# The S5 stretch of a hybrid diffusion layer, issued to TensorE in a written order

## The chip, the cores and the metric

The kernel runs on one core of a Trainium2 chip. Times are device microseconds of one execution. The kernel before took 1824.79 us, the median of 3 runs (1820.09 to 1827.46). A core has TensorE (PE, matrix products), VectorE (DVE), ScalarE (ACT), GpSimd (POOL) and SyncE (SP, which issues the transfers); each engine executes its own queue in order, and they wait for each other by semaphores.

## The reference, cut to what matters

One layer of a diffusion backbone over 256 context tokens and 512 latent tokens, width 1024, all in float32. One projection feeds three mixers:

```
hc, h = norm(context), norm(latent)             # (256, 1024), (512, 1024)
proj  = h @ w_in        # u (S5) | q,k,v | beta, decay | z | conv value, conv gate | gates
u     : s5_scans(u)     # 64 groups x 64 complex states, both directions, context then latent
        y = Re(C h) + d*u ; gelu(y) * sigmoid(gelu(y) @ w_glu)
q,k,v : silu(conv of 3 taps); q,k divided by their norm; gated delta rule, chunks of 64, both directions
conv  : value*sigmoid(gate); conv of 31 taps; layernorm; silu
merged = sum of three sigmoid gates * (branch @ w_br) ; x + g1 * (merged @ w_out)
then a ConvGLU feed-forward and a last norm
```

The context rows need only the states of S5 and the delta rule, so of u, q, k, v there are 768 columns (512 + 256), of conv 512.

## The kernel before, in words

Matrices are kept transposed: 128 channels on the partitions, tokens along the row. `proj` (L406) makes 128 channels: it loads 8 weight tiles, splits them into a high and a low part (`split`, high on ACT L181, low on DVE or POOL L185), and `mm3` runs 24 matmuls (L206 to L208) into one PSUM bank; with the context another 24 of 256 columns follow.

S5 is handled in 8 blocks of 8 groups. For a block:

- `s5_u` projects u (on PE) and sends it to DRAM; `s5_in` reads it back as `s5U`.
- `s5_in` makes input weights on DVE (`cmul`, L170 to L175, each 128x1024), transposes them on PE (L600, copied by ACT L602), multiplies them with `s5U` (L610) and has ACT copy the result to `s5VH` (L612 to L614); K matmuls (L628) and two transposes (L634) make the local kernel, which goes to DRAM.
- `s5_phase` and `s5_scan` run on GpSimd: the phase table (`s5ph`, powers by doubling), six products over 128x768 (L648, `s5G`), 16 scans on DVE (L658), six products over 128x512 (`s5H`). The tables `s5ph`, `s5G`, `s5H`, `s5pt` have one buffer each, so the loop of the blocks is closed on GpSimd.
- `s5_y` makes output weights on DVE (L686 to L691), copies H (ACT L694, L695) and runs 8 x (1 matmul of L699, 2 of L702); the page counts each of the 24 as two records.

Behind the stretch of S5 the program has `dn_gates` (the decay gates, a long chain of small DVE operations between its transposes, L1068, and its sums, L1109), `conv_in` (for each of 8 channel tiles two projections and `conv_taps`: 32 matmuls, 64 records, L939, with four loads of `cv_y` and a weight tile that GpSimd makes) and `dn_pre` (for each of 8 heads: K, Q, V by `proj`, `dn_silu` on DVE and ACT, transposes L1165, L1176, L1193, norms). Then the delta rule begins (`dn_head`, first matmul L1240); it is filled up with `jobs` (L738 to L743), projections that are cut in single matmuls.

The order on each engine is not the order of the code: a scheduler places every instruction by priority (code order) and readiness. Projections of later blocks and of `dn_pre` so come between the S5 steps wherever the scheduler found room. Buffers come from pools: `dn_th` (two buffers) holds silu's temporaries, and the conv input `cv_t` too, whose edges GpSimd clears (L888, L889).

Of the kernel before, what the change touches and what calls it, by code (L numbers as in the profile page):

```python
# [16 lines left out]
P = 128  # L17
# [62 lines left out]
class Kern:  # L80
# [337 lines left out]
    def s5_u(self, m, pool):  # L418
# [6 lines left out]
        nc.sync.dma_start(self.u_d[m], st.rearrange("p j n -> p (j n)"))  # L425

# [143 lines left out]
    def s5_in(self, blk, NG=8):  # L570
# [5 lines left out]
        U = bp.tile([P, NG, 96], F32, name="s5U")  # L576
        ud = self.u_d[blk]
        for j in range(8):
            nc.sync.dma_start(
                U[16 * j:16 * j + 16],  # L580
                bass.AP(tensor=ud.tensor, offset=ud.offset + j * 96, ap=[[768, 16], [16 * 768, NG], [1, 96]]))
# [11 lines left out]
        self.cmul(w[0], w[1], bv[0], bv[1], av[0], av[1], t)  # L593
        WT = []
# [9 lines left out]
        VH = bp.tile([P, 2, NG, 96], F32, name="s5VH", tag="s5VH", bufs=2)  # L604
# [11 lines left out]
        zd = self.dp.tile([240, 16 * NG], F32, name=f"z_d{blk}")  # L616
# [14 lines left out]
        nc.scalar.activation(kt.rearrange("p h f -> p (h f)"), ps[:, :2 * P], AF.Copy)  # L631
        ps = self.psum(tag="s5")
# [8 lines left out]
        return U, VH, zd  # L641

    def s5_scan(self, blk, st, T, NG=8):
# [3 lines left out]
        VH = st[1]  # L647
# [12 lines left out]
        H = self.s5b.tile([P, 2, NG, 64], F32, name="s5H", bufs=1)  # L660
# [7 lines left out]
        return H  # L668

    def s5_y(self, blk, st, H, NG=8):  # L670

        nc, V = self.nc, self.nc.vector
        U, _, z = st
# [17 lines left out]
        V.tensor_tensor(w[1], w[1], t, op=OP.subtract)  # L691

# [181 lines left out]
    def conv_in(self, pool, cvp):  # L874

# [6 lines left out]
        self.conv_weights(cvp)  # L882
        for m in range(KT):
            yield
# [5 lines left out]
            nc.scalar.activation(mid, pg, AF.Tanh, scale=0.5)  # L890
            pa = self.proj(COL_CV + m * P)
# [4 lines left out]
        yield  # L896
        self.conv_taps(KT - 1, cvp)
        nc.sync.dma_start(self.sm_d, self.cv_sm)
# [150 lines left out]
    def dn_gates(self, pool):  # L1049
# [4 lines left out]
        self.rq = cp.tile([P, HEADS, NX], F32, name="rq")  # L1054
        self.rqx = cp.tile([P, HEADS, NX], F32, name="rqx")
# [60 lines left out]
    def dn_silu(self, part, h, pool, c0, out=None):  # L1116
# [17 lines left out]
        V.tensor_scalar(a, raw[:, a0:W], w(0), None, op0=OP.mult)  # L1134
# [14 lines left out]
    def dn_pre(self, h, pool):  # L1149
# [5 lines left out]
        cols = lambda n: self.psum(tag="aux")[:, :n * P].rearrange("p (c f) -> p c f", f=P)  # L1155
        kqt = pool.tile([P, 2 * NX, P], F32, name="dn_Hw", tag="dn_Hw", bufs=2)
        kq = kqt.rearrange("p (c a) f -> p c a f", a=2)
        t, th = self.dn_silu(1, h, pool, COL_K)
# [3 lines left out]
        for c0, c1 in halves:  # L1162
            pt = cols(c1 - c0)
            for c in range(c0, c1):
                nc.tensor.transpose(pt[:, c - c0], t[:, self.tok(c)], self.ident)  # L1165
                nc.scalar.activation(th[:, self.tok(c)], pt[:, c - c0], AF.Square, accum_out=x[:, c:c + 1])
            pts.append(pt)
        V.tensor_scalar(x, x, 4.0 * EPS, None, op0=OP.add)
        self.rsqrt(r, x, pool, NCH, h == HEADS - 1)
        kt = pool.tile([P, NCH + NCT, P], F32, name="dn_Hw", tag="dn_Hw", bufs=2)  # L1170
# [9 lines left out]
        t, th = self.dn_silu(0, h, pool, COL_Q, out=kq[:, :, 1])  # L1180
        sq = th[:, NCTX + 1:]
        nc.scalar.activation(sq.rearrange("p (c f) -> p c f", f=P), kq[:, :, 1], AF.Square)
        ps = self.psum(tag="aux")
        for c in range(NX):
            nc.tensor.matmul(ps[:, c:c + 1], sq[:, c * P:(c + 1) * P], self.ones[:, :1], start=True, stop=True)
# [619 lines left out]
```

## Time and profile before

| | |
|---|---|
| median of 3 runs | 1824.79 us (1820.09 to 1827.46) |
| profiled execution | 1821.67 us, span of its instructions 1819.9 us |
| mean granted TensorE clock | 0.939 |
| PE busy | 1650.5 us, 91% of the span |
| DVE, POOL, ACT busy | 1159.9, 819.0, 691.1 us |
| first projection / last matmul of S5 / first matmul of the delta rule | 50 / 570 / 724 us |

Busy time on PE holds matmuls at the lower clock as well, and matmuls overlap: the time that one takes in a stream is the distance of starts, not its duration. A release `<-ACT x` names what ended the idle time ahead of a row.

### The profile page before, as it was taken

What the parts mean: (1) busy time and instruction counts of PE and PEld (TensorE: products, weight loads), DVE (VectorE), ACT (ScalarE), POOL (GpSimd) and SP (SyncE); (2) the same over time, 40 slices, a digit from 0 to 9 for tenths busy, and PEclk for the clock granted to TensorE, in tenths of its full rate; (3) what the DMA queues carried; (4) which work ended last, traced back from release to release, by engine and by line L of the source; (5) the groups of instructions that cost most, each with busy time, mean ns of one, the idle gap of its engine ahead of it and who ended that gap; (6) DMA issues with size and microseconds to landing.
All of it is one profiled execution on the core that took longest, in us unless ns stands there. A gap on an engine that the chain in (4) does not pass through costs nothing.

```text
span 1819.9 us, 25815 instructions
## 1 busy us (share of the span) xinstructions
PE 1650.5 (91%) x9435; PEld 1339.1 (74%) x9435; DVE 1159.9 (64%) x1982; ACT 691.1 (38%) x1398; POOL 819.0 (45%) x978
## 2 busy tenths in 40 slices
PE   7899878898989999988979989999699799999997
PEld 2687767787878366766768878888567688888886
DVE  6746897678886064366776466544245699999424
ACT  4444433543443144333334455444213243334222
POOL 0548886788782323876455445433142111111020
PEclk9899988988899999998988999999889899999999
DMA  8342332333236668777776455656784233333232
GB/s 297 97 108 77 76 100 83 85 98 94 74 104 164 175 180 286 219 221 218 239 240 164 133 177 158 173 178 190 240 287 150 70 105 93 93 99 99 94 97 76
DMA packets 328689, 268.71 MB, mean 148 GB/s; under 512 B 63333, under 2 KB 264818, under 8 KB 328562
## 3 DMA queue, kind: packets, MB, share of 16 engines
q1 hardware_dynamic: 328130, 266.52, 49.4%
q8 instruction: 74, 1.21, 0.3%
q10 hardware_dynamic: 432, 0.54, 0.1%
q14 instruction: 53, 0.43, 0.1%
HBM read 208.62 MB, written 58.39 MB: 147 GB/s over the span
## 4 chain that ended last, share of the span: by engine, by line
PE 39%; DMA 6%; DVE 4%; POOL 2%; ACT 2%; issue 2%; SPq 0%; DVEq 0%; ACTq 0%; POOLq 0%
PE ps_mm L206 5%; PE ps_mm L207 5%; PE ps_mm L208 5%; PE ps_pr L1240 3%; PE ps_acc L1522 3%; PE ps_mm L738 3%; PE ps_mm L743 3%; PE ps_mm L742 3%; PE ps_acc L1523 3%; PE ps_acc L1521 3%; PE ps_inv L1240 2%; DMA adw<-in_ada_w_dram 1%; DVE kkc L1284 1%; POOL dn_tmp L1303 1%; POOL dn_dd L1305 1%
## 5 line engine op out<-in xcount | busy, mean ns | idle before, releaser
L181 ACT ACTIVATE whi<-wraw 128x1024 fp32r<-128x1024 f32 x187 | 196.8, 1055 | 362.0 <-PE ps_mm L207 167.3
L185 DVE TENSOR_TENSOR wlo<-wraw,whi 128x1024 fp32r<-128x1024 f32 x131 | 177.1, 1354 | 184.5 <-ACT whi L181 184.1
L185 POOL TENSOR_TENSOR wlo<-wraw,whi 128x1024 fp32r<-128x1024 f32 x56 | 135.0, 2412 | 160.3 <-ACT whi L181 152.4
L206 PE MATMUL ps_mm<-hxh,whi 128*128 128x512 f32 (+1 forms) x392 | 160.9, 411 | 11.3 <-ACT dn_raw L1126 8.7
L208 PE MATMUL ps_mm<-hxh,wlo 128*128 128x512 f32 (+1 forms) x392 | 158.5, 404 | 3.1 <-DVE wlo L185 3.1
L207 PE MATMUL ps_mm<-hxl,whi 128*128 128x512 f32 (+1 forms) x392 | 159.2, 406 | 0.7 <-POOL hxl L404 0.7
L1620 DVE SCALAR_TENSOR_TENSOR f_acc<-fpad,vec,f_acc 128x512 f32<-128x512 f32 x176 | 152.5, 866 | 3.2
L185 POOL TENSOR_TENSOR hidl<-f_acc,hidh 128x512 fp32r<-128x512 f32 x22 | 36.8, 1672 | 240.8 <-ACT hidh L181 240.8
L206 PE MATMUL ps_mm<-h2h,whi 128*128 128x512 f32 x352 | 137.7, 392 | 0.7 <-ACT h2h L1585 0.7
L207 PE MATMUL ps_mm<-h2l,whi 128*128 128x512 f32 x352 | 137.5, 391 | 0.0
L208 PE MATMUL ps_mm<-h2h,wlo 128*128 128x512 f32 x352 | 137.3, 390 | 0.0
L743 PE MATMUL ps_mm<-hxh,wlo 128*128 128x512 f32 x256 | 104.7, 409 | 3.5 <-POOL wlo L185 3.4
L738 PE MATMUL ps_mm<-hxh,whi 128*128 128x512 f32 x256 | 106.8, 418 | 0.0
L742 PE MATMUL ps_mm<-hxl,whi 128*128 128x512 f32 x256 | 103.2, 403 | 0.0
L206 PEld LDWEIGHTS ps_mm<-hxh,whi 128*128 128x128 f32 (+1 forms) x392 | 76.0, 194 | 27.3 <-ACT dn_raw L1126 9.2
L208 PEld LDWEIGHTS ps_mm<-hxh,wlo 128*128 128x128 f32 (+1 forms) x392 | 75.4, 192 | 21.2 <-DVE wlo L185 3.7
L207 PEld LDWEIGHTS ps_mm<-hxl,whi 128*128 128x128 f32 (+1 forms) x392 | 75.9, 194 | 15.5 <-POOL hxl L404 1.2
L702 PE MATMUL ps_s<-s5HB,s5w 128*128 128x64 f32 x256 | 57.2, 360 | 28.5 <-DVE s5w L691 20.0
L742 PE MATMUL ps_mm<-xl,whi 128*128 128x512 f32 x192 | 77.8, 405 | 0.8 <-DVE xl L185 0.8
L206 PEld LDWEIGHTS ps_mm<-h2h,whi 128*128 128x128 f32 x352 | 66.5, 189 | 14.8 <-ACT h2h L1585 1.1
L743 PE MATMUL ps_mm<-xh,wlo 128*128 128x512 f32 x192 | 77.3, 404 | 0.0
L738 PE MATMUL ps_mm<-xh,whi 128*128 128x512 f32 x192 | 76.4, 406 | 1.0 <-ACT xh L181 1.0
(504 smaller groups left out, 4412.2 us busy)
## 6 DMA issues: line engine op xcount, KB each, us to landing
wraw<-in_w_in_dram SPq DMA_DIRECT2D x80, 512.0 KB
wraw<-in_ffn_w_up_dram SPq DMA_DIRECT2D x44, 512.0 KB
adw<-in_ada_w_dram SPq DMA_DIRECT2D x32, 512.0 KB
wraw<-in_ffn_w_down_dram SPq DMA_DIRECT2D x22, 512.0 KB
cv_y<-cvi SPq DMA_DIRECT2D x32, 270.0 KB
adaw<-in_ada_w_dram SPq DMA_DIRECT2D x16, 512.0 KB
h_d<-dn_Hw SPq DMA_DIRECT2D x16, 384.0 KB
dn_Hb<-h_d SPq DMA_DIRECT2D x8, 768.0 KB
```

Of the source, the lines that this page charges most:

```text
L181: nc.scalar.activation(hi, x, AF.Copy, scale=scale)
L185: (nc.vector if lo_eng == "V" else nc.gpsimd).tensor_tensor(lo, x, hi, op=OP.subtract)
L206: T.matmul(ps, wh[:, k], xh[:, k], start=first and k == 0, stop=False)
L207: T.matmul(ps, wh[:, k], xl[:, k], start=False, stop=False)
L208: T.matmul(ps, wl[:, k], xh[:, k], start=False, stop=last and k == n - 1)
L702: nc.tensor.matmul(py[:, g], w[i][:, g].rearrange("p t c -> p (t c)"), HB[:, i, g], start=False, stop=i == 1)
L738: i = T.matmul(ps, wh[:, k], xh[:, k], start=k == 0, stop=False)
L742: T.matmul(ps, wh[:, k], xl[:, k], start=False, stop=False)
L743: T.matmul(ps, wl[:, k], xh[:, k], start=False, stop=k == KT - 1)
L1240: self.dn_mm = T_.matmul(*a, **kw)
L1521: nc.tensor.matmul(ps[i], xh, wh[:, e], start=k == 0, stop=False)
L1620: V.scalar_tensor_tensor(acc, pad[:, i:i + R, j:j + W], w(t), acc, op0=OP.mult, op1=OP.add)
```

## The change

The S5 stretch becomes one function, `s5_all`, inside a region in which TensorE keeps the order of the code (`tc.manual_schedule`); the other engines are scheduled as before. Its steps are generators, advanced one step at a time. In iteration b: projection of u of block b+1; transposes of the input weights of block b; one piece of `fill`; VH and K matmuls of b; one piece; transposes of K; one piece (two from b = 5); the 24 matmuls of y of block b-1; then phase and input weights of b+1 and one more piece.

`fill` is `dn_inputs`: for each head five pieces, each one or two projections (K; Q; conv gate; V; conv value) with the transposes, norms and sums that belong to them, V's transposes one piece later. It has 41 pieces, of which 38 run inside the stretch. `conv_in` keeps only the projections; all `conv_taps`, `conv_weights` and `dn_gates` come behind the stretch. The first tap of `dn_silu` moves from DVE to ACT. The sums of q's squares use another PSUM bank. The three K, Q, V silus keep their buffers, in another order.

```diff
@@ dn_silu
-        V.tensor_scalar(a, raw[:, a0:W], w(0), None, op0=OP.mult)
+        nc.scalar.activation(a, raw[:, a0:W], AF.Copy, scale=w(0))
@@ s5_y and the other steps: yield at each border
         V.tensor_tensor(w[1], w[1], t, op=OP.subtract)
+        yield
@@ new
+    def s5_all(self, pool, fill):
+        st = [{} for _ in range(KT)]
+        f = lambda n=1: [next(fill, None) for _ in range(n)]
+        st[0]["U"] = self.s5_u(0, pool)
+        x = self.s5_in(0, st[0])
+        next(x)
+        T = self.s5_phase(0)
+        f(2)
+        for b in range(KT + 1):
+            if b + 1 < KT:
+                st[b + 1]["U"] = self.s5_u(b + 1, pool)
+            if b < KT:
+                next(x)
+                f()
+                next(x)
+                z = self.s5_scan(b, st[b], T)
+                next(z)
+            if b:
+                y = self.s5_y(b - 1, st[b - 1])
+                next(y)
+            if b < KT:
+                f()
+                next(x)
+            f(2 if b > 4 else 1)
+            if b:
+                next(y)
+            if b < KT:
+                next(z)
+            if b + 1 < KT:
+                T = self.s5_phase(b + 1)
+                x = self.s5_in(b + 1, st[b + 1])
+                next(x)
+                f()
@@ conv_in
-    def conv_in(self, pool, cvp):
+    def conv_in(self, pool):
...
-            if m:
-                self.conv_taps(m - 1, cvp)
...
+    def conv_mid(self, pool):
+        self.conv_weights(pool)
+        for m in range(KT):
+            self.conv_taps(m, pool)
+            yield
+        self.nc.sync.dma_start(self.sm_d, self.cv_sm)
@@ new
+    def dn_inputs(self, pool):
+        cv = self.conv_in(pool)
...
+        last = iter(())
+        for h in range(HEADS):
+            x = self.dn_pre(h, pool)
+            next(x)
+            next(last, None)
+            yield
+            next(x)
+            yield
+            next(cv)
+            next(x)
+            yield
+            next(x)
+            yield
+            next(cv)
+            next(x)
+            yield
+            last = x
+        next(last)
+        yield
@@ the kernel's body
-                            st = {}
-                            for b in range(KT + 1):
-                                if b < KT:
-                                    k.s5_u(b, dq)
-                                    st[b] = k.s5_in(b)
-                                if b:
-                                    h = k.s5_scan(b - 1, st[b - 1], k.s5_phase(b - 1))
-                                    k.s5_y(b - 1, st[b - 1], h)
+                        fill = k.dn_inputs(dq)
+                        with k.rpool("s5b", 3) as k.s5b, k.rpool("s5w") as k.s5w, \
+                                tc.manual_schedule(engines={nc.tensor.engine}):
+                            k.s5_all(dq, fill)
+                        with k.rpool("cvp") as cvp:
+                            cv = k.conv_mid(cvp)
+                            for _ in fill:
+                                next(cv)
                             k.dn_gates(dq)
-                        with k.rpool("cvp") as cvp:
-                            cv = k.conv_in(dq, cvp)
-                            next(cv)
-                            for h in range(HEADS):
-                                k.dn_pre(h, dq)
-                                next(cv, 0)
+                            for _ in cv:
+                                pass
                             k.dn_qnorm(cvp)
-                            next(cv, 0)
```

How instructions stand on TensorE around the third block's K transposes (`s5K`) and the y matmuls of the block ahead (`s5HB` with `s5w`, and `s5U` with `s5TG`), before:

```order
L634 MATMUL ps_s_1514<-ident,s5K 128x128 [waits Activation_49]
L699 MATMUL ps_s_1627<-s5U,s5TG 128x64 [waits PE_49]
...
L206 MATMUL ps_mm<-hch,whi 128x256
L702 MATMUL ps_s_1627<-s5HB,s5w_1613 128x64 [waits DVE_49]
L207 MATMUL ps_mm<-hcl,whi 128x256
L1165 MATMUL ps_aux<-ident,dn_s 128x128 [waits Activation_49]
...
L207 MATMUL ps_mm<-hxl,whi 128x512
L702 MATMUL ps_s_1627<-s5HB,s5w_1614 128x64 [waits DVE_49]
L699 MATMUL ps_s_1627<-s5U,s5TG 128x64
L702 MATMUL ps_s_1627<-s5HB,s5w_1613 128x64
```

And in the changed kernel, where L640, L707, L710 and L1215 are the former L634, L699, L702 and L1165:

```order
L640 MATMUL ps_s_2529<-ident,s5K 128x128 [waits Activation_49]
L206 MATMUL ps_mm<-hxh,whi 128x512
...
L208 MATMUL ps_mm<-hxh,wlo 128x512
L1215 MATMUL ps_aux<-ident,dn_s 128x128 [waits DVE_49]
L1215 MATMUL ps_aux<-ident,dn_s 128x128 x5
L707 MATMUL ps_s_2603<-s5U,s5TG 128x64 [waits PE_49]
L710 MATMUL ps_s_2603<-s5HB,s5w_2474 128x64 [waits DVE_49]
L710 MATMUL ps_s_2603<-s5HB,s5w_2475 128x64 [waits DVE_49]
L707 MATMUL ps_s_2603<-s5U,s5TG 128x64
...
L710 MATMUL ps_s_2603<-s5HB,s5w_2475 128x64
L206 MATMUL ps_mm<-hxh,whi 128x512 [waits Activation_49]
```

Before, the first matmul of y, and single ones of the others, stand far ahead of the rest of the 24, each with a wait for DVE, and pieces of projections between them. Now 24 projection matmuls and six transposes of K stand between the K transposes of S5 and y, and the 24 of y are together.

GpSimd, in the middle of the operations of a block, where the edges of `cv_t` are cleared; before:

```order
L648 TENSOR_TENSOR s5H<-s5H,s5pt 128x512 [waits Pool_49]
L648 TENSOR_TENSOR s5pt<-s5G,s5ph 128x8x64 [waits Pool_49]
L888 MEMSET cv_t 128x15 [waits DMAHW5_49,DVE_49]
L889 MEMSET cv_t 128x16
L648 TENSOR_TENSOR s5H<-s5H,s5pt 128x512 [waits Pool_49]
L549 MEMSET s5ph 128x8
```

And in the changed kernel, in the second block:

```order
L654 TENSOR_TENSOR s5G<-s5G,s5pt 128x768 [waits Pool_49]
L654 TENSOR_TENSOR s5pt<-s5VH,s5ph 128x768 [waits Pool_49]
L930 MEMSET cv_t 128x15 [waits DVE_49,PE_49,Activation_49]
L931 MEMSET cv_t 128x16
L654 TENSOR_TENSOR s5G<-s5G,s5pt 128x768 [waits Pool_49]
L654 TENSOR_TENSOR s5H<-s5G,s5ph 128x512 [waits DVE_49]
```

The memset waited for a transfer and DVE before, and now waits for TensorE and ACT as well; the six products of `s5G` and `s5H` stand behind it. Seven of the eight memsets of the changed kernel wait for TensorE, none did before.

TensorE at the gates, their transposes of `g_bd` and their first sum (`G` with `U`); before:

```order
L208 MATMUL ps_mm<-hxh,wlo 128x512
L1068 MATMUL ps_aux<-ident,g_bd 128x32 [waits Activation_49]
...
L208 MATMUL ps_mm<-hxh,wlo 128x512
L1109 MATMUL ps_aux<-G,U_74 128x48 [waits DVE_49]
L1109 MATMUL ps_aux<-G,L_76 128x48
```

And in the changed kernel, where L986 are the conv taps, L1113 and L1154 the former L1068 and L1109:

```order
L1113 MATMUL ps_aux<-ident,g_bd 128x32 [waits Activation_49]
L1113 MATMUL ps_aux<-ident,g_bd 128x32 x5
L986 MATMUL ps_s_6321<-cv_y,cv_d 32x512 x12
L986 MATMUL ps_s_6365<-cv_y,cv_d 32x512 [waits DMAHW3_49,DMAHW2_49,DMAHW7_49,DMAHW0_49,Pool_49]
L986 MATMUL ps_s_6365<-cv_y,cv_d 32x512 x31
L783 MATMUL ps_mm<-hxh,whi 128x512
...
L986 MATMUL ps_s_6409<-cv_y,cv_d 32x512 [waits DMAHW2_49,DMAHW3_49,DMAHW0_49,DMAHW7_49,Activation_49,Pool_49]
L986 MATMUL ps_s_6409<-cv_y,cv_d 32x512 x31
L1154 MATMUL ps_aux<-G,U_74 128x48 [waits DVE_49]
L1154 MATMUL ps_aux<-G,L_76 128x48
```

Before, 145 instructions of S5 and projections stand between the two; now 12 + 32 + 32 matmuls of the conv taps and four of the jobs. Ahead of the first matmul of the delta rule there are now 48 matmuls of the jobs, 119 before; after 78 matmuls of `dn_head` both kernels have had 429, and the order behind that is nearly the same.

## Rows read from the trace of the kernel before

**Rows 1.** per stage: window, length, busy us (count) of each engine, clock, DMA share

```profile
50.00:112.00 62.00, 57.03 (x335) 48.66 (x336) 40.80 (x66) 28.97 (x51) 31.67 (x51) 0.90 0.38 99
112.00:570.00 458.00, 407.49 (x2864) 357.69 (x2863) 362.33 (x538) 188.23 (x414) 349.93 (x430) 0.90 0.33 92
570.00:724.00 154.00, 146.31 (x948) 88.19 (x948) 56.42 (x99) 52.04 (x107) 45.05 (x38) 0.98 0.72 203
724.00:1300.00 576.00, 526.13 (x3154) 451.65 (x3153) 323.01 (x626) 238.90 (x565) 304.07 (x395) 0.95 0.65 192
```

**Rows 2.** TensorE groups, 50 to 724 us: count, busy us, mean ns, idle before

```profile
L206 PE MATMUL ps_mm<-hxh,whi 128*128 128x512 f32 x384 | 157.8, 411 | 11.3 <-ACT dn_raw L1126 8.7 <-ACT hxh L403 2.4 <-ACT cv_t L890 0.2
...
L939 PE MATMUL ps_s<-cv_y,cv_d 128*32 128x512 f32 x512 | 61.2, 608 | 4.0 <-DMA cv_y<-cvi 4.0
L206 PE MATMUL ps_mm<-hch,whi 128*128 128x256 f32 x192 | 58.9, 307 | 2.0 <-ACT dn_raw L1129 1.8
...
L702 PE MATMUL ps_s<-s5HB,s5w 128*128 128x64 f32 x256 | 57.2, 360 | 28.5 <-DVE s5w L691 20.0 <-DVE s5w L688 4.5 <-DVE dn_raw L1123 4.1
```

**Rows 3.** timeline of TensorE: start, duration, line, tiles, count [idle before]

```profile
99.65 0.28 PE L206 MATMUL ps_mm<-hch,whi 128*128 128x256 f32 x1
...
100.00 0.28 PE L206 MATMUL ps_mm<-hch,whi 128*128 128x256 f32 x1
...
295.38 0.63 PE L207 MATMUL ps_mm<-hxl,whi 128*128 128x512 f32 x1
...
296.67 0.63 PE L207 MATMUL ps_mm<-hxl,whi 128*128 128x512 f32 x1
...
321.15 0.39 PE L206 MATMUL ps_mm<-hxh,whi 128*128 128x512 f32 x1
...
322.51 0.39 PE L206 MATMUL ps_mm<-hxh,whi 128*128 128x512 f32 x1
...
568.67 0.39 PE L699 MATMUL ps_s<-s5U,s5TG 128*128 128x64 f32 x2
569.34 0.39 PE L699 MATMUL ps_s<-s5U,s5TG 128*128 128x64 f32 x2
...
724.02 0.60 PE L1240 MATMUL ps_prep<-dn_Hk 128*128 128x128 f32 x4
```

**Rows 4.** waits of TensorE, 120 to 560 us: total, times, longest

```profile
PE ps_s L702 <- DVE s5w L691: 20.0, 4, 6.3
PE ps_s L600 <- DVE s5w L172: 7.0, 2, 5.9
```

**Rows 5.** timeline of GpSimd (POOL), first block and fifth

```profile
123.75 1.84 POOL L648 TENSOR_TENSOR s5G<-s5VH,s5ph 128x768 f32<-128x768 f32 x1 [25.30 <-ACT s5VH L614]
...
307.24 2.32 POOL L648 TENSOR_TENSOR s5H<-s5H,s5pt 128x512 f32<-128x512 f32 x1
...
312.82 0.11 POOL L549 MEMSET s5ph<- 128x8 f32 x1
...
343.61 1.85 POOL L648 TENSOR_TENSOR s5G<-s5VH,s5ph 128x768 f32<-128x768 f32 x1 [7.15 <-ACT s5VH L614]
...
347.22 2.83 POOL L648 TENSOR_TENSOR s5G<-s5VH,s5ph 128x768 f32<-128x768 f32 x1
```

**Rows 6.** waits of GpSimd, 120 to 560 us

```profile
POOL s5G L648 <- ACT s5VH L614: 51.7, 6, 25.3
POOL s5pt L648 <- DVE s5G L658: 19.7, 7, 4.4
POOL s5H L648 <- DVE s5G L658: 16.8, 8, 3.2
```

**Rows 7.** groups of VectorE instructions by line, 100 to 570 us

```profile
L1134 DVE TENSOR_SCALAR dn_s<-dn_raw,vec 128x769 f32<-128x769 f32 x13 | 11.9, 917 | 0.1
```

**Rows 8.** timeline of TensorE, the gates' transposes and sums

```profile
165.62 0.55 PE L1068 MATMUL ps_aux<-ident,g_bd 32*128 32x32 f32 x6
...
205.15 0.32 PE L1109 MATMUL ps_aux<-G,U 128*128 128x48 f32 x2
```

More of the change, by code (lines that the diff above doesn't have):

```diff
@@ L425, in s5_u @@
         nc.sync.dma_start(self.u_d[m], st.rearrange("p j n -> p (j n)"))
+        U = self.s5b.tile([P, 8, 96], F32, name="s5U")
+        ud = self.u_d[m]
+        for j in range(8):
+            nc.sync.dma_start(
+                U[16 * j:16 * j + 16],
+                bass.AP(tensor=ud.tensor, offset=ud.offset + j * 96, ap=[[768, 16], [16 * 768, 8], [1, 96]]))
+        return U
     def s5_prep(self, pool):
@@ L568, in s5_powers, with s5_in @@
         return t, [ps[:, i, :, :, None].to_broadcast([P, NG, 8, 16]) for i in range(2)]
-    def s5_in(self, blk, NG=8):
+    def s5_in(self, blk, st, NG=8):
         nc, V = self.nc, self.nc.vector
@@ L575, in s5_in @@
         lo, hi = slice(0, 64), slice(64, P)
[L576 to L581, printed above, removed]
         cd = self.cd
@@ L603, in s5_in @@
             WT.append(t)
-        VH = bp.tile([P, 2, NG, 96], F32, name="s5VH", tag="s5VH", bufs=2)
+        yield
+        U = st["U"]
+        VH = st["VH"] = bp.tile([P, 2, NG, 96], F32, name="s5VH", tag="s5VH", bufs=2)
         for h in range(NG // 2):
@@ L614, in s5_in @@
             nc.scalar.activation(ov[hi, :, :, 32:], pv[hi, :, :, 95:31:-1], AF.Copy)
-        zd = self.dp.tile([240, 16 * NG], F32, name=f"z_d{blk}")
+        zd = st["z"] = self.dp.tile([240, 16 * NG], F32, name=f"z_d{blk}")
         ps = self.psum(tag="s5")
@@ L667, in s5_scan, with s5_y @@
             tt(H[:, i], H[:, i], t, op)
-        return H
-    def s5_y(self, blk, st, H, NG=8):
+        yield
+    def s5_y(self, blk, st, NG=8):
         nc, V = self.nc, self.nc.vector
-        U, _, z = st
+        U, H, z = st["U"], st["H"], st["z"]
         wp = self.s5w
@@ L890, in conv_in @@
             nc.scalar.activation(mid, pg, AF.Tanh, scale=0.5)
+            yield
             pa = self.proj(COL_CV + m * P)
@@ L1155, in dn_pre @@
         cols = lambda n: self.psum(tag="aux")[:, :n * P].rearrange("p (c f) -> p c f", f=P)
+        t, th = self.dn_silu(1, h, pool, COL_K)
+        yield
         kqt = pool.tile([P, 2 * NX, P], F32, name="dn_Hw", tag="dn_Hw", bufs=2)
         kq = kqt.rearrange("p (c a) f -> p c a f", a=2)
-        t, th = self.dn_silu(1, h, pool, COL_K)
+        _, thq = self.dn_silu(0, h, pool, COL_Q, out=kq[:, :, 1])
+        sq = thq[:, NCTX + 1:]
+        nc.scalar.activation(sq.rearrange("p (c f) -> p c f", f=P), kq[:, :, 1], AF.Square)
+        yield
         x = pool.tile([P, NCH], F32, name="dn_x", tag="dn_x", bufs=2)
@@ L1165, in dn_pre @@
                 nc.tensor.transpose(pt[:, c - c0], t[:, self.tok(c)], self.ident)
+            for c in range(c0, c1):
                 nc.scalar.activation(th[:, self.tok(c)], pt[:, c - c0], AF.Square, accum_out=x[:, c:c + 1])
@@ L1169, in dn_pre @@
         self.rsqrt(r, x, pool, NCH, h == HEADS - 1)
+        yield
+        tv, _ = self.dn_silu(2, h, pool, COL_V)
+        ps = self.psum(tag="s5")
+        for c in range(NX):
+            nc.tensor.matmul(ps[:, c:c + 1], sq[:, c * P:(c + 1) * P], self.ones[:, :1], start=True, stop=True)
+        V.tensor_scalar(self.rqx[:, h], ps[:, :NX], 4.0 * EPS, None, op0=OP.add)
+        yield
         kt = pool.tile([P, NCH + NCT, P], F32, name="dn_Hw", tag="dn_Hw", bufs=2)
@@ L1179, in dn_pre @@
         nc.sync.dma_start(hd[:, 12:14], kc)
[L1180 to L1185, printed above, removed]
-        V.tensor_scalar(self.rqx[:, h], ps[:, :NX], 4.0 * EPS, None, op0=OP.add)
         nc.sync.dma_start(hd[:, 14:22], kqt)
-        t, th = self.dn_silu(2, h, pool, COL_V)
+        yield
         vtok = pool.tile([P, NCH, P], F32, name="dn_Hw", tag="dn_Hw", bufs=2)
@@ L1192, in dn_pre @@
             for c in range(c0, c1):
-                nc.tensor.transpose(pt[:, c - c0], t[:, self.tok(c)], self.ident)
+                nc.tensor.transpose(pt[:, c - c0], tv[:, self.tok(c)], self.ident)
             nc.scalar.activation(vtok[:, c0:c1], pt, AF.Copy, scale=0.5)
         nc.sync.dma_start(hd[:, 6:12], vtok)
+        yield
+    def dn_inputs(self, pool):
+        cv = self.conv_in(pool)
+        self.rq = self.cp.tile([P, HEADS, NX], F32, name="rq")
+        self.rqx = self.cp.tile([P, HEADS, NX], F32, name="rqx")
+        last = iter(())
[3 more added lines that the diff above has]
+            next(last, None)
+            yield
+            next(x)
+            yield
+            next(cv)
+            next(x)
+            yield
+            next(x)
+            yield
+            next(cv)
+            next(x)
+            yield
+            last = x
+        next(last)
+        yield
     def dn_qnorm(self, pool):
```

15 lines of the change are left out of this document (4 added, 11 removed).

## The prediction

> **What bounds the kernel now.** I read the busy times by stage first. From 50 us, where the first projection starts, to 724 us, where the delta rule starts, TensorE is busy 57.03 + 407.49 + 146.31 = 610.8 of 674 us, at a granted clock of 0.90 up to 570 us [rows 1]. Behind 724 us the instructions stand nearly as before, so the question is how long this stage lasts with the same work in it.
>
> Busy time at 0.90 holds matmuls that ran slowly, so next come the starts in the timeline. [...] Six records of y take 569.34 - 568.67 = 0.67 us [rows 3]. The counts by line give the work of the stage at the upper clock: 3 x 384 x 0.227 = 262 for projections of the latent rows, 3 x 192 x 0.117 = 67 for those of the context, 61 for the conv taps, 384 records x 0.112 = 43 for y [rows 2, 3], 119 job matmuls = 27, and by my estimate 90 for the rest (VH, transposes, K, norms, gates), priced by counts and the same speeds. That is 550 us of work in 674: 124 us are lost, 63 of them idle and some 60 to the lower clock.
>
> What makes the gaps: y's matmuls wait 20.0 us for their weights on VectorE, the transposes of the input weights 7.0 us in the same way [rows 4]. Behind them stands GpSimd's loop over the blocks. It waits 51.7 us for VH, 25.3 of it in the first block, and 19.7 + 16.8 for VectorE's scans [rows 6].
>
> **The stretch after the change.** Nothing is taken off TensorE but the place of 119 - 48 = 71 job matmuls: 71 x 0.227 = 16 us go behind 724 us, where TensorE is busy 526 of 576 us [rows 1] and they cost their full time. Everything else is a matter of what fills the gaps. In the written order the work at the upper clock is 46 us up to the first VH, 396 from there to the last y (49.5 per block, 56 where a block has five pieces of fill), and 97 from there to the delta rule (70 + 48 projection matmuls, 61 of taps, 48 jobs and small ones): 539 us.
>
> The first VH cannot be much earlier than now, since its weights are made on VectorE while GpSimd waits until 123.75 [rows 5]: I take 112 us for it, so that 62 - 46 = 16 us are lost up to it.
>
> From there three engines compete for the period of a block. TensorE needs 49.5 to 56. VectorE is busy 362 of 458 us now [rows 1]; the first taps leave it (24, where 13 of the long form took 11.9 us [rows 7], so 19 us in all, and ScalarE with 188 of 458 us busy takes them in its gaps), the gates leave, and about five more silus come in, so 46 per block. GpSimd is busy 350 us with eight scans and seven phases [rows 1]; the phase of the fifth block took 343.61 - 7.15 - 312.82 = 23.6 us [rows 5], so a turn costs (350 + 24)/8 = 46.7 us, and with (19.7 + 16.8)/8 = 4.6 us of waiting for scans [rows 6] 51.3. This loop is closed, as its tables have one buffer each, so it is the floor for the middle blocks. On top comes the wait for VH: the later five waits are now (51.7 - 25.3)/5 = 5.3 us each [rows 6], and the denser TensorE makes them no shorter; I take 5.7 for every turn. The price of this wait lies between 0 (VH always early) and 15 (a VectorE queue in the wrong order); the nearest row is the present one. So the period is 57 us. The same reckoning gives (569 - 45 - 124)/7 = 57 for now [rows 3, 5], with the 45 us explained next: I expect the loop to keep its pace and TensorE to do more work beside it.
>
> Seven periods bring the last VH to 112 + 399 = 511. Behind it come five pieces of fill and y(6), some 45 us, in which also the last scan ends (twelve operations, some 23 us, and the waits of rows 6). The last y ends at 556, now 570; the time lost between the first VH and it is 556 - 112 - 396 = 48 us. What goes: the waits of rows 4, since y's weights are due after two or three pieces of fill, and with the idle time the pieces at the lower clock. What is late next: VH for GpSimd and, on VectorE, scans that stand behind silus.
>
> **The end of the stage.** 97 us of work, and two things in its way. The gates' transposes and sums stood 205.15 - 165.62 = 40 us apart [rows 8] with other work in between; now 152 records of taps and four jobs, 19 us, cover a VectorE chain that cannot be shorter than its own operations, some 45 small ones, by my estimate 27 us together: 8 us of stall, between 0 (a shorter chain) and 40 - 19 = 21 (the present distance). And the transfers: 570 to 724 us has a DMA share of 0.72 [rows 1], 111 us of transfers, which do not fit below 111 us unless some of them move behind. I take 14 us for both. So 111 us, where the end now takes 154 - 16 = 138 without those jobs: this is most of the gain, since all but three of the 41 pieces are done before it. The delta rule starts at 556 + 111 = 667.
>
> **The sum.** 724 - 16 - 667 = 41 us gained. The profiled execution took 1821.67 us, so 1781; the median of the runs shown lies 3.1 us above it: 1784 us.
>
> **Unsure places.** The memsets of `cv_t` now wait for TensorE in seven of eight cases, in GpSimd's queue; the steps that they wait for (K's transposes and squares of a head) come one piece, 24 x 0.227 = 5.5 us or more, before the piece that needs the buffer. I price them at nothing beyond the 5.7 us above, since TensorE is not behind GpSimd there; were TensorE late by a piece at each, 7 x 5.5 = 39 us would go to the loop. The first tap on ScalarE puts an operation ahead of each tanh: nothing to 24 x 0.9 = 22 us, hidden, as ScalarE is busy 41% of the stretch.
>
> GpSimd's operation over 128x768 took 1.85 us once and 2.83 us in the same turn, with VectorE busy beside it [rows 5]. [...]
>
> **Rivals.**
>
> 1. The queues stretch each other: each of the three engines is wanted for 80 to 90% of a period, a late step of one is passed on, and the period rises to 60. Then the last VH is at 532, y at 577, the delta rule at 688, gain 20: 1805. About the same comes out if transfers hold the end of the stage at its 138 us behind 556 (694, gain 14: 1811). For it: a fixed order cannot pass a late operand by, as the scheduler's mixture did. Against: the y and transposes that wait now get two or three pieces of cover. 0.22.
> 2. No wait beyond GpSimd's floor: period 52.5, y at 525, 105 us behind it, delta rule at 630, gain 78: 1747. For it: 25.3 of the 51.7 us are the first block alone. 0.16.
> 3. Slower: GpSimd's twelve scan operations all run beside VectorE. Six at 2.83 and six at 2.32 us [rows 5] are 30.9 us, where the mean is (350 - 7 x 23.6)/8 = 23; the phase rises with them by perhaps 3. The period is then 51.3 + 8 + 3 + 5 = 67: y at 112 + 469 + 45 = 626, delta rule at 737, 29 us lost: 1854. The point from which it decides is 708 = 112 + 7p + 45 + 111, so p = 63. For it: VectorE's load per us rises. Against: it rises only from 79 to 81%. 0.1.
> 4. The order is not what decides, and what the stretch gains is lost to stalls in front of the delta rule: within half a per cent of before, 1815 to 1825. 0.05.
>
> **How the numbers follow.** The forecast (periods of 55 to 58.5 us, 1770 to 1795) has 0.47. Half a per cent, 9 us, is about what a measurement of this kernel can tell from no change. Faster: 0.47 + 0.16 + most of rival 1 (0.21) = 0.84; same: 0.07; slower: 0.09. The range leaves out the faster half of rival 2, rival 3 and the slow part of rival 4: 1748 to 1813.
>
> **What would show it.** Right: the last y near 556 us, no waits of y for its weights above 1 or 2 us, the clock of the stretch at 0.95 or more, GpSimd's turns at 57 us with waits for VH of about 6 us, the delta rule at 667, and a stall of some 8 us at the gates' sums. The step on the period is wrong if the turns take 60 or more: then GpSimd's row at 768 columns shows whether its operations are slower (rival 3) or its waits longer (rival 1). The step on the end is wrong if the taps wait for `cv_y`. The whole is wrong if TensorE waits for VectorE at the input weights' transposes of each block, at half clock behind it.

## The result, and the profile after

The changed kernel takes 1794.51 us in the median of 4 runs (1790.74 to 1799.76), the kernel before 1823.39 beside it (1820.09 to 1827.46): a ratio of 0.984 with a 95% interval of 0.981 to 0.988, so 28.9 us faster. The forecast was 1784 us. The profiled execution took 1797.43 us, with a span of 1795.6 against 1819.9, 24.3 us less, and it loses them ahead of the delta rule: that starts at 683.8 instead of 724.0, 40 us earlier, 16 of which are the job matmuls that now stand behind it.

The stages, as in [rows 1]: window, length, busy us (count) of TensorE, its weight loads, VectorE, ScalarE and GpSimd, then the clock and the DMA share.

```profile
50.00:115.00 65.00, 55.01 (x298) 45.21 (x299) 44.58 (x67) 32.02 (x55) 32.88 (x51) 0.87 0.32 82
115.00:578.00 463.00, 422.83 (x3058) 372.54 (x3056) 356.41 (x506) 216.38 (x477) 348.18 (x433) 0.95 0.37 103
578.00:684.00 106.00, 96.42 (x723) 47.36 (x722) 39.16 (x103) 32.45 (x62) 35.44 (x32) 0.98 0.81 221
684.00:1300.00 616.00, 554.99 (x3255) 472.28 (x3255) 332.08 (x641) 247.01 (x576) 316.71 (x402) 0.94 0.66 201
```

From 50 us to the delta rule TensorE is now busy 55.0 + 422.8 + 96.4 = 574.3 of 634 us, before 610.8 of 674. Idle time is nearly what it was, 60 us against 63. Of the 36.5 us of busy time that are gone 16 are the moved jobs; the other 20 fit the granted clock, which is 1.00 or 0.50 in both traces. At 0.50 TensorE is busy for 47.9 us between 50 us and the delta rule, before 89.6, and half of the difference, by estimate what it saves, is 20.8; the mean of the stretch is 0.95 instead of 0.90. Which waits went and which came is in the groups of TensorE (50 to 684 us; count, busy us, mean ns, idle before it and what ended it):

```profile
L206 PE MATMUL ps_mm<-hxh,whi 128*128 128x512 f32 (+1 forms) x392 | 162.6, 415 | 1.9 <-ACT hxh L403 1.9
...
L710 PE MATMUL ps_s<-s5HB,s5w 128*128 128x64 f32 x256 | 39.1, 275 | 0.0
...
L603 PE MATMUL ps_s<-ident,s5w 128*128 128x128 f32 x128 | 23.2, 339 | 35.2 <-ACT s5WT L605 19.4 <-DVE dn_raw L1168 5.9 <-DVE s5w L175 5.5
```

The matmuls of y, L702 before [rows 2], waited 28.5 us and took 57.2; now they wait for nothing and take 39.1. In their place the transposes of the input weights (L603) wait 35.2 us, where they waited 8.5 us before, 7.0 of it in one line of [rows 4]. More than half of it is a wait for ScalarE's copies out of PSUM. One of them in the timeline of TensorE, then the last matmuls of y and the first of the delta rule, which answer to the last lines of [rows 3]:

```profile
390.73 1.03 PE L603 MATMUL ps_s<-ident,s5w 128*128 128x128 f32 x8
396.76 1.97 PE L603 MATMUL ps_s<-ident,s5w 128*128 128x128 f32 x8 [5.00 <-ACT s5WT L605]
...
577.74 0.61 PE L710 MATMUL ps_s<-s5HB,s5w 128*128 128x64 f32 x4
...
683.79 0.95 PE L1318 MATMUL ps_prep<-dn_Hk 128*128 128x128 f32 x4 [3.57 <-DMA dn_Hk<-h_d]
```

Eight transposes take 1.03 us, then TensorE idles for 5.00, and the next eight take 1.97: the granted clock is 1.00 from 390.7 to 391.8 us and 0.50 from 396.7 to 398.8. ScalarE's own timeline shows what it did meanwhile:

```profile
385.76 1.06 ACT L702 ACTIVATE s5HB<-s5H 64x1024 f32<-64x1024 f32 x1 [2.59 <-POOL s5H L654]
...
392.98 0.63 ACT L1182 ACTIVATE dn_th<-dn_s 128x512 f32<-128x512 f32 x1 [2.58 <-DVE dn_s L1181]
393.51 0.58 ACT L424 ACTIVATE ust<-ps_mm 128x512 f32<-128x512 f32 x1
394.38 0.63 ACT L1207 ACTIVATE dn_th<-dn_Hw 128x512 f32<-128x512 f32 x1 [0.28 <-DVE dn_raw L1168]
394.91 1.04 ACT L181 ACTIVATE whi<-wraw 128x1024 fp32r<-128x1024 f32 x1
395.86 0.36 ACT L423 ACTIVATE ust<-ps_mm 128x256 f32<-128x256 f32 x1
396.12 1.08 ACT L605 ACTIVATE s5WT<-ps_s 128x512 f32<-128x512 f32 x2
```

The first copy could have run at about 391.3, when its four transposes were done (an estimate, half of the 1.03 us). It stands behind a silu's tanh that waits for VectorE's taps, and behind four more operations. In this trace the copy did not pass the tanh: ScalarE sat idle for 2.58 us, from 390.40 until 392.98, while the transposes of a copy behind the tanh were done at about 391.3. Over the stretch this tanh is ScalarE's largest wait, and GpSimd's is still the one for VH, 48.3 us against 51.7 in [rows 6]:

```profile
ACT dn_th L1182 <- DVE dn_s L1181: 94.1, 17, 13.4
```

```profile
POOL s5G L654 <- ACT s5VH L619: 48.3, 8, 10.5
```

VectorE in the same turn, its queue from the weights of y to the silu behind the scans:

```profile
361.34 2.87 DVE L695 TENSOR_TENSOR s5w<-s5w,s5t 128x1024 f32<-128x1024 f32 x1
364.25 1.22 DVE L697 TENSOR_TENSOR s5t<-cc,ps_pw 128x1024 f32<-128x1024 f32 x1
...
365.99 1.22 DVE L698 TENSOR_TENSOR s5w<-s5w,s5t 128x1024 f32<-128x1024 f32 x1
367.12 2.87 DVE L185 TENSOR_TENSOR wlo<-wraw,whi 128x1024 fp32r<-128x1024 f32 x1
369.91 6.80 DVE L664 TENSOR_TENSOR_SCAN s5G<-r,s5G 128x96 f32<-128x96 f32 x16
376.63 1.20 DVE L185 TENSOR_TENSOR wlo<-wraw,whi 128x1024 fp32r<-128x1024 f32 x1
377.75 4.05 DVE L1181 SCALAR_TENSOR_TENSOR dn_s<-dn_raw,vec,dn_s 128x769 f32<-128x769 f32 x2
```

So a turn reads as one chain (turn 4, VH at 349.9 us): VH's copies until 357.5, GpSimd's six operations for G until 371.7, beside them VectorE's weights of y, the scans until 376.7, the taps of a silu behind them until 381.8, further weights and taps until 392.9, ScalarE's tanh, the copies of the next block's weights until 399.4, fill, and the next VH at 405.7: 55.8 us.

The end of the stage: the gates' transposes and sums, [rows 8] before, are 23 us apart and not 40, with a stall of 3.0. By stages, the gain is here: the last y ends 8 us later than before (578 for 570), and from there to the delta rule it takes 105 us instead of 154, 16 of which are the moved jobs.

```profile
628.69 0.55 PE L1113 MATMUL ps_aux<-ident,g_bd 32*128 32x32 f32 x6
...
651.83 0.42 PE L1154 MATMUL ps_aux<-G,U 128*128 128x48 f32 x2 [3.04 <-DVE G L1146]
```

### The profile page after: what moved, and what is told of

Same layout as the page of the kernel before. It is cut to its first block, busy times and chain, and to the rows that moved or that the text cites. A ratio compares the mean times of both kernels' runs of the same rounds, so it can differ in the third digit from the quotient of the medians.

```text
span 1795.6 us, 25808 instructions
## 1 busy us (share of the span) xinstructions
PE 1634.2 (91%) x9435; PEld 1324.1 (74%) x9435; DVE 1143.3 (64%) x1958; ACT 706.8 (39%) x1422; POOL 815.2 (45%) x978
## 4 chain that ended last, share of the span: by engine, by line
PE 58%; DVE 17%; DMA 12%; issue 5%; ACT 5%; POOL 3%; SPq 1%; DVEq 0%; ACTq 0%; POOLq 0%
PE ps_mm L206 9%; PE ps_mm L207 9%; PE ps_mm L208 8%; PE ps_pr L1318 4%; DMA adw<-in_ada_w_dram 3%; PE ps_mm L783 3%; PE ps_mm L788 3%; PE ps_mm L787 3%; PE ps_acc L1600 3%; PE ps_acc L1601 3%; PE ps_acc L1599 3%; PE ps_inv L1318 2%; DVE wlo L185 2%; DVE ad_acc L321 2%; DVE s5G L664 2%
## 5 line engine op out<-in xcount | busy, mean ns | idle before, releaser
L181 ACT ACTIVATE whi<-wraw 128x1024 fp32r<-128x1024 f32 (+1 forms) x187 | 196.6, 1054 | 379.1 <-PE ps_mm L207 195.6
L185 DVE TENSOR_TENSOR wlo<-wraw,whi 128x1024 fp32r<-128x1024 f32 (+1 forms) x131 | 179.7, 1374 | 173.6 <-ACT whi L181 173.0
L207 PEld LDWEIGHTS ps_mm<-h2l,whi 128*128 128x128 f32 x352 | 66.6, 189 | 13.9
```

The source lines that it names most:

```text
L181: nc.scalar.activation(hi, x, AF.Copy, scale=scale)
L185: (nc.vector if lo_eng == "V" else nc.gpsimd).tensor_tensor(lo, x, hi, op=OP.subtract)
L207: T.matmul(ps, wh[:, k], xl[:, k], start=False, stop=False)
```

## The experiments

Each was timed beside the kernel before. "VH(7)" is the distance from the first VH to the eighth in the timeline of the profiled execution, "y" the end of the last y, "delta" the start of the delta rule, all in us. The last three are of one execution each; VH(7) differs by 5 us between the changed kernel and e1, whose edit was expected to change nothing.

| kernel | median | ratio to before, 95% | VH(7) | y | delta |
|---|---|---|---|---|---|
| before | 1823.4 | | 395 | 570 | 724 |
| changed | 1794.5 | 0.984 (0.981 to 0.988) | 407 | 578 | 684 |
| e1 room | 1788.7 | 0.980 (0.976 to 0.983) | 403 | 582 | 697 |
| e2 both | 1787.4 | 0.979 (0.974 to 0.983) | 401 | 574 | 684 |
| e3 weights only | 1817.2 | 0.996 (0.994 to 0.998) | 426 | 606 | 720 |
| e4 no written order | 1796.5 | 0.984 (0.981 to 0.987) | 398 | 574 | 684 |
| e5 before, tap and gates | 1805.1 | 0.990 (0.988 to 0.993) | 387 | 557 | 711 |
| e6 before, gates | 1818.0 | 0.997 (0.995 to 0.999) | 397 | 569 | 721 |
| e7 tap on VectorE | 1814.5 | 0.994 (0.992 to 0.997) | 418 | 592 | 700 |
| e8 copies on VectorE | 1792.2 | 0.984 (0.981 to 0.987) | 402 | 581 | 697 |
| e9 phase once | 1791.0 | 0.982 (0.978 to 0.986) | 405 | 576 | 684 |
| e10 VectorE lean | 1801.8 | 0.987 (0.983 to 0.991) | 406 | 587 | 699 |
| e11 lean, no order | 1791.8 | 0.982 (0.979 to 0.985) | 397 | 587 | 694 |
| e12 table once | 1788.8 | 0.981 (0.979 to 0.983) | 392 | 572 | 686 |

Before, e5 and e6 have 71 to 72 jobs (16 us) more ahead of the delta rule. Its start is not the whole time either: from there to the start of its last product with its state (`ps_pr` from `dn_S`) it takes 586 us in the changed kernel, e4 and e7, but 567 to 570 in e1, e8 and e11, with the same jobs ahead of it, 571 to 582 in the other changed kernels and 570 in the kernel before. So e1 starts it 13 us after the changed kernel and ends 4 us ahead of it in the profiled executions. Why this stage takes up to 19 us more in some of the kernels, no run shows.

**Buffers: e1, e2, e3.** First theory: the transposes' waits come from the weight buffers, which input and output weights share, so that one block's weights are made only after the other's are read. e1 makes the room that this takes and is the control; e3 gives the output weights their own buffers, e2 also the products' temporary.

```
-        VH = st["VH"] = bp.tile(..., tag="s5VH", bufs=2)
+        VH = st["VH"] = bp.tile(..., tag="s5VH", bufs=1)              # e1, e2, e3
-        T = wp.tile(..., tag="s5T")     ...   Y = wp.tile(..., tag="s5t")
+        T = wp.tile(..., tag="s5HB")    ...   Y = wp.tile(..., tag="s5HB")
-        w = [wp.tile(..., name=f"s5w{i}") for i in range(2)]          # in s5_y
+        w = [wp.tile(..., name=f"s5v{i}") for i in range(2)]          # e2, e3
-        t = self.s5w.tile(..., tag="s5WT", bufs=2)                    # in s5_powers
+        t = self.s5w.tile(..., tag="s5tt")                            # e2
```

> The changed kernel with 12 KB per partition freed for the next runs: one buffer instead of two for s5VH, and s5T, s5HB and s5Y in one buffer. Nothing in the stretch should need them apart (VH is read 12 us after it is written and made anew 58 us later). Every theory: as the changed kernel, 1794.5 us within 6, last y near 578 us, period of the VH matmuls 58 us. If it is slower by more than 6 us, these buffers are part of what sets the pace.

> As e1_room, with the output weights in buffers of their own (s5v0, s5v1 instead of s5w0, s5w1) and the temporary s5t in a buffer of its own. Theory 1, a closed loop through the weights' single buffers sets the pace (K matmuls of b, output weights of b-1 on VectorE, y of b-1, input weights of b+1, their transposes, VH and K of b+1; 58 us a turn, with 35 us of TensorE waiting at the transposes over the stretch): those waits fall under 10 us, the pace falls to GpSimd's own 52 to 54 us, last y near 545 us, 1764 us (1755 to 1775). Rival 2, VectorE's queue is full and late whatever the buffers: as the changed kernel, 1788 to 1800 us, the waits at the transposes stay above 25 us. Rival 3, GpSimd's loop already sets the pace: no change either, but GpSimd's waits for VH fall to nothing.

> As e2_both, but s5t stays in the two buffers that it shares with the transposed weights. Theory 1 in its strong form (each shared buffer closes the loop by itself): most of the gain of e2_both is missing, 1785 to 1796 us. Theory 1 in its weak form (the weights' buffers alone close it): as e2_both. Rival 2: as the changed kernel.

e1 came as expected (5.8 us faster than the changed kernel, intervals that overlap). e2 is no faster than e1 (their intervals nearly coincide), and the wait for the copies has not gone; it was 12.4 us in e1 and 19.4 in the changed kernel, and all waits of L603 together are 26.6, 28.4 and 35.2 us in e2, e1 and the changed kernel:

```profile
PE ps_s L603 <- ACT s5WT L605: 19.1, 7, 5.8
```

The theory falls. e3 is 28 us slower than e1, which no expectation had. In its trace GpSimd's memsets of `cv_t` wait 56.9 us for the squares of K (21.7 in the changed kernel), 34.8 of them from 120 us on, where e1 has 16.0, and VH(7) is 24 us longer than in e1. What makes it so is not shown; that the buffers changed the order of the work in VectorE's queue is a guess.

**The written order: e4.** The changed kernel without the `manual_schedule` line.

```
-                        with k.rpool("s5b", 3) as k.s5b, k.rpool("s5w") as k.s5w, \
-                                tc.manual_schedule(engines={nc.tensor.engine}):
+                        with k.rpool("s5b", 3) as k.s5b, k.rpool("s5w") as k.s5w:
```

> The changed kernel without the region that keeps TensorE's order, so the scheduler places the same code. Theory A, the gain comes from doing nearly all projections inside the stretch and the written order only arranges them: 1790 to 1805 us, work moves with the code. Theory B, the kept order makes the gain: back to 1812 to 1826 us, with waits of y for its weights of 15 us or more again.

It takes the same time, as theory A had it, though the waits that theory B named came back: y waits for its weights again (18.3 us together, as the 20.0 + 4.5 of before), the transposes hardly.

```profile
PE ps_s L710 <- DVE s5w L698: 9.8, 5, 3.8
PE ps_s L710 <- DVE s5w L695: 8.5, 5, 4.6
```

So the kept order of TensorE's steps, which is what the change says of itself, brings nothing here; it trades one wait for another. VH(7) is even 9 us shorter without it, as again in e11 against e10. The gain must lie in what came with it.

**The smaller edits: e5, e6, e7.** e6 is the kernel before with the gates moved behind the blocks (two tiles that `dn_pre` needs are therefore made ahead of it), e5 has the first tap on ScalarE as well. e7 is the changed kernel with the tap back on VectorE.

```
-                                k.dn_gates(dq)                        # e5, e6: in the block loop
...
+                                if h == HEADS - 1:
+                                    k.dn_gates(dq)                    # ahead of the last dn_pre
                                 k.dn_pre(h, dq)
-        V.tensor_scalar(a, raw[:, a0:W], w(0), None, op0=OP.mult)     # e5; the other way in e7
+        nc.scalar.activation(a, raw[:, a0:W], AF.Copy, scale=w(0))
```

> The kernel before with only dn_gates moved behind the blocks, ahead of the last head's dn_pre. Theory 3 says that the gates' share is in proportion to their VectorE time, 27 of 46 us: 12 to 18 us gained, 1805 to 1811. Rival (the gates already stood in gaps of VectorE): 1820 to 1826. If they are faster here than in the run with both edits, the tap on ScalarE costs.

> The kernel before, in its own code order and under the scheduler, with two of the smaller edits alone: the first tap of the delta rule's convs on ScalarE instead of VectorE, and dn_gates emitted only ahead of the last head's dn_pre instead of between the blocks. Theory 3 (the gain is VectorE relieved during the stretch: 19 us of taps and some 27 us of gates leave it): most of the gain appears without the rewritten stretch, 1795 to 1805 us, the delta rule near 690 to 700. Rival (the gain is the new order of projections and blocks, which gives TensorE work beside each wait): at most a third of the gain, 1813 us or more.

> The changed kernel with one edit undone: the first tap of the delta rule's convs on VectorE again (24 operations, 19 us in all). Theory 3: VectorE sets the pace of the stretch, so it is 8 to 19 us slower than the changed kernel, 1802 to 1813. Rival (VectorE is not behind, and ScalarE's queue, which gets shorter by 24 operations, is what holds the transposes' copies up): no change or some us faster, 1787 to 1797, and the waits of the input weights' transposes for ScalarE fall below 12 us.

The gates bring 5.5 us, less than expected. The tap brings 12.9 in the old order and 20.0 in the new one, and the intervals of each pair lie apart. So e5, at the edge of theory 3's range, has 18 of the 29 us without the rewritten stretch; e7 lies 1.5 us above its own. What is left for the rewritten code order (fill, late conv taps, the other PSUM bank, the order of the silus; not tested apart) is 3.5 us without the tap (e6 to e7), where the intervals overlap, and 10.6 with it (e5 to changed), where they lie just apart. The rewritten order moves time from the end of the stage into the stretch: from e6 to e7 the last y ends 23 us later, and the delta rule starts 21 us earlier, 16 of them the moved jobs. In e6 TensorE's transposes of K wait for a silu on VectorE, a wait that the kernel before does not have; in e5 it is nearly gone. The line of e6, then that of e5 (120 to 560 us):

```profile
PE ps_aux L1163 <- DVE dn_s L1137: 40.3, 7, 10.0
```

```profile
PE ps_aux L1163 <- DVE dn_s L1137: 4.5, 3, 2.5
```

The operation itself, on VectorE in e7 and on ScalarE in the changed kernel ([rows 7] had 917 ns; in e6, with the gates moved, it is 1351 in the 12 from 115 to 520 us):

```profile
L1179 DVE TENSOR_SCALAR dn_s<-dn_raw,vec 128x769 f32<-128x769 f32 x14 | 19.1, 1364 | 0.0
```

```profile
L1179 ACT ACTIVATE dn_s<-dn_raw,vec 128x769 f32<-128x769 f32 x14 | 13.3, 949 | 0.1
```

**Which engine holds the copies: e8.** Buffers of e1, and the copies on VectorE.

```
-                nc.scalar.activation(t[:, 4 * h:4 * h + 4], ps.rearrange(...), AF.Copy)
+                V.tensor_copy(t[:, 4 * h:4 * h + 4], ps.rearrange(...))
```

> The changed kernel with the buffers as in e1, and the four PSUM copies per block of the transposed input weights on VectorE instead of ScalarE. Theory 2 (TensorE waits for these copies since they stand in ScalarE's queue behind a silu's tanh that waits for VectorE): the waits of the transposes, 19 us for the copies, fall below 5, all waits in that line below 12, and the time is 1770 to 1780. Rival (VectorE is as late as ScalarE, and the wait only takes another name): waits of 20 us or more in that line, 1785 to 1800.

The rival was right: same time as e1 within the intervals, the same VH(7), and the wait has another name (all waits of L603 are 32.2 us, 28.4 in e1).

```profile
PE ps_s L603 <- DVE s5WT L605: 17.6, 6, 5.5
```

**GpSimd's share: e9.** The prediction's floor, tested by taking 7 x 23.6 us off GpSimd.

```
-                T = self.s5_phase(b + 1)
```

> The changed kernel without seven of the eight table computations on GpSimd (s5_phase for block 0 only, its table used by all blocks, so the values of y in the later blocks are left out): some 7 x 23.6 = 165 us less work on GpSimd. Theory A, the prediction's (GpSimd's closed loop is the floor of the period, 51.3 us): the period falls to TensorE's 50 to 52 us, the last y comes 40 us or more earlier, 1750 to 1760. Theory B (VectorE's queue sets the pace and GpSimd follows it): GpSimd waits for VH for most of what it no longer works, the period stays at 55 or more, 1780 to 1792. Theory C (B, and VectorE is slow because GpSimd works beside it): the second and third tap over 128x769, 1.69 us now, fall towards the 1.0 us of their fastest, VectorE loses 20 to 35 us, 1762 to 1778.

Theory B: VH(7) goes from 407 to 405 us, and GpSimd waits for nearly all that it no longer works, 85 us more for VH (133.0 for 48.3) and 65 more in the memsets of `cv_t`, for TensorE's VH matmuls. Theory C falls as well, since the second and third tap take 1.69 us as before (mean of 28 in both traces); GpSimd still has the products of G and H, and is busy 195.5 us from 115 to 560 us.

```profile
POOL s5G L654 <- ACT s5VH L619: 133.0, 8, 31.5
POOL cv_t L929 <- PE ps_s L615: 66.6, 3, 24.7
```

**VectorE's load: e10, e11, e12.** e12 makes the masked table once (buffers of e1), e10 also moves the scaling of K's tokens to ScalarE, e11 is e10 without the written order.

```
-        dg = bp.tile([P, NG, 16], F32, name="s5dg", bufs=1)   # and its DMA and product
+        dg = self.dg[:, g0:g0 + NG]                           # made once in s5_prep
-            V.tensor_tensor(ktok[:, c0:c1], pt, r[:, c0:c1, None].to_broadcast(...), op=OP.mult)
+            for c in range(c0, c1):                           # e10, e11
+                nc.scalar.activation(ktok[:, c], pt[:, c - c0], AF.Copy, scale=r[:, c:c + 1])
```

> The changed kernel with the buffers of e1, the masked table s5dg made once ahead of the stretch instead of once per block (7 x 1.56 = 10.9 us of VectorE in the stretch), and the scaling of K's tokens by r on ScalarE, 48 operations instead of 16 on VectorE (7.1 us). Theory 3 (each us that leaves VectorE in the stretch is worth about one, as 19 us of taps were worth 20): 14 to 18 us faster than e1's 1788.7, 1770 to 1775. Rival (ScalarE, with 13 us more, now holds up the copies out of PSUM that TensorE waits for, or GpSimd is the floor): 1784 to 1795.

> The kernel of e10 without the written order of TensorE's steps, that is under the scheduler. Theory 3 (the order of TensorE decides nothing as long as VectorE sets the pace): within 4 us of e10. Rival (once VectorE is relieved, the fixed order is what lets TensorE go at its pace): 8 us or more slower than e10.

> The kernel of e10 with one of its two edits alone: the masked table s5dg made once ahead of the stretch (10.9 us of VectorE leave it, nothing is added to ScalarE); K's tokens are scaled on VectorE again; buffers as in e1. Theory 3 (VectorE's busy time sets the pace, and e10 was slower only for ScalarE's longer queue): 9 to 11 us faster than e1's 1788.7, 1777 to 1780. Theory D (the pace is a closed chain through the queues' order: VH, GpSimd's six operations for G, the scans in VectorE's queue, the taps behind them, ScalarE's tanh, behind it the copies of the next block's weights, the next VH; the masked table stands beside GpSimd's six operations, so taking it away makes the scans wait for G instead): at most 4 us, 1785 to 1790, and the scans' wait for G, 1.7 us now, rises to 8 us or more.

e10 is 13 us slower than e1, where theory 3 had it 14 to 18 faster, and outside the rival's range too. e12 says why: against it, e10 has 7.8 us less on VectorE and 11.6 more on ScalarE, and its VH(7) is 406 instead of 392, its time 13.0 us more. The moved operations also wait 24.9 us for r, at the head of ScalarE's queue:

```profile
L1232 ACT ACTIVATE dn_Hw<-ps_aux,dn_r 128x128 f32<-128x128 f32 x42 | 11.6, 375 | 27.5 <-DVE dn_r L115 24.9 <-DVE dn_raw L1168 2.6
```

Neither theory has e12 whole. By the median it is level with e1, as D expected, and the scans wait for G, 8.6 us where e1 has 3.4:

```profile
DVE s5G L664 <- POOL s5G L654: 8.6, 5, 1.7
```

But in the trace VH(7) is 10 us shorter than in e1, as theory 3 had it, and the delta rule starts 11 us earlier. The table's products took 8.9 us of VectorE in e1 (the 10.9 are those of the changed kernel), and VectorE's busy time between the first and the last VH falls by 5.6. The delta rule's stage is then 6 us longer (574 instead of 568, measured as below the table), and the rest of the difference between the two profiles, 4.7 us of span, is within what the runs scatter. Why the delta rule gives most of it back I did not find out; e1's stage is one of the short ones named there. e11 is 10 us faster than e10 by the medians, which neither expectation had; their intervals just overlap, so that the fixed order costs something here is likely and not shown.

## Why the prediction was right, and where it was not

**The time** lay in the range, 10.5 us above the forecast, and inside the forecast's own 1770 to 1795. The term that carried it held: the end stage, said to be most of the gain, was to fall from 138 us without the jobs to 111 and took 105.5, and the moved jobs cost 16 us behind it in the changed kernel, as forecast. But two of the steps on the stretch were wrong, and the landmarks are those of the first rival (y at 577, delta rule at 688, 1805 us) rather than the forecast's 556 and 667: measured are 578 and 684. That the time still came within the forecast is in part luck: the profiled executions lie 24 us apart, which from 1824.8 would give 1801, and the medians of the runs 29.

**The floor of the period (wrong).** The step took GpSimd's closed loop, 51.3 us and 5.7 of waiting, for the period. The period is 407/7 = 58.2 us, near the 57 forecast, but not for that reason: with 165 us less work for GpSimd it is 57.9 (e9). The traces point to the chain above, in which VectorE and ScalarE take turns: copy, tap, taps, tanh, product, and behind these the next block's copies. The runs price its links, each from one profiled execution: 11.6 us more on ScalarE, with the waits that they bring, cost 14 in VH(7) (e10 against e12), 8.9 us of products taken off VectorE save 10 (e12 against e1), the tap on VectorE costs 10.4 (e7), a copy moved from one to the other nothing (e8), seven of GpSimd's eight tables 2 (e9). That the chain closes through the order of the queues is read from the timeline and agrees with these prices; no run broke it open, so it is argued and not shown. Of the rivals it is the first, a late step passed on, with a period below its 60 us.

**The first taps (mis-sized).** The prediction put them into VectorE's load of 46 us per block and left them out of the sum, as GpSimd was to be slower. They are the largest single item, 13 to 20 of the 29 us. It called them hidden on ScalarE, and there they were. Without them there the last y is at 592 us (e7), and what the end stage gains is nearly all lost in the stretch.

**The order of TensorE's steps (wrong as the cause).** The prediction let the pieces of fill between a step and its operand take the waits of y away, and with them the lower clock. They went as forecast (from 50 us to the delta rule the clock is 0.50 for 64.1 us, before 115.1), but e4 has the time without the order. The prediction named the sign that would make the whole wrong, TensorE waiting at the input weights' transposes with half clock behind it. It came, 35.2 us, 19.4 of them for ScalarE instead of VectorE, with a clock of 0.50 behind the wait shown at 396.76, and took back what y's waits had given; the time held all the same, since the end stage carried it.

**Sizes.** First VH 115 instead of 112; seven periods 407 instead of 399; from VH(7) to the last y 56 instead of 45, so that this part took as long as any turn; so y at 578 and not 556, 22 us late. The end stage took 105.5 and not 111, with 3.0 us of stall at the gates for 8. Together 17 us, the 41 forecast less the 24 measured in the profile. The 539 us of work that the sum starts from are 5 more than its own 550 less the 16 that move away, which the prediction does not explain. The projection matmuls in these sums, 0.227 us for 512 columns and 0.117 for 256, are priced by distances of starts in [rows 3], (322.51 - 321.15)/6 and (100.00 - 99.65)/3, at a granted clock of 1.00; at 0.50 three of 512 took 296.67 - 295.38 = 1.29 us, 0.43 each.

**Right:** the end stage as the place of the gain; the clock of the stretch, 0.95; no waits of y for its weights; the memsets of `cv_t` in the changed kernel, whose one long wait of 21.7 us ends at 117.1 us, while GpSimd's products can begin only at 121.8, when the first VH is copied; all of the gain ahead of the delta rule.

## What to carry to other kernels

When a rewritten order comes with small moves between engines, take these out one by one first: here moving 24 small operations from VectorE to ScalarE was worth 13 to 20 of 29 us, and the kept order of TensorE itself nothing. A period that several engines with idle time share need not be the time of one of them; follow one turn from wait to wait, and price each link by adding or removing a few us there. If a fixed order frees one operand, look what stands in the queue ahead of the operand that is due next.

## What the runs showed of the hardware

In the turn shown, VectorE and GpSimd read as if they took turns where both operands of VectorE's operation lie in SBUF. In the fence of VectorE's queue the sum at 361.34, with both operands in SBUF, took 2.87 us, the product at 364.25, with one operand in PSUM, 1.22. GpSimd in the same turn of the changed kernel:

```profile
361.23 1.90 POOL L654 TENSOR_TENSOR s5G<-s5VH,s5ph 128x768 f32<-128x768 f32 x1
363.09 2.84 POOL L654 TENSOR_TENSOR s5G<-s5G,s5pt 128x768 f32<-128x768 f32 x1
366.01 2.90 POOL L654 TENSOR_TENSOR s5pt<-s5VH,s5ph 128x768 f32<-128x768 f32 x1
368.99 2.70 POOL L654 TENSOR_TENSOR s5G<-s5G,s5pt 128x768 f32<-128x768 f32 x1
```

GpSimd's operation ends at 361.23 + 1.90 = 363.13, VectorE's sum 1.08 us later, at 364.21; GpSimd's next ends at 365.93, 1.72 us behind that. The same at the next pair: GpSimd ends at 368.91, VectorE's `wlo` at 369.99, 1.08 later, GpSimd at 371.69, 1.70 later. In between VectorE's L698, with both operands in SBUF, came first: it took its 1.22, ended at 367.21, and the GpSimd operation that started with it took 2.90 and ended 1.70 later. So each looks as if it ran only when the other was done, and the duration that the profile gives holds the wait: 2.87 for the 1.20 that `wlo` takes at 376.63, 2.84 for the 1.85 of [rows 5]. In this turn that is as strong as an exclusion; no run of its own tested it. By this reading VectorE's busy time holds time in which it waits for GpSimd. The third rival, in which slower operations of GpSimd cost 29 us, did not come: GpSimd is busy 348 us in the stretch, as the 350 of before.
